# A Strassen-type encoder layer on one core: four turned copies and one row scaling on VectorE, one weight's conversion behind the sums of h, three behind bank copies

## The chip, the core and the metric

One core of a Trainium2 chip runs the whole kernel. It has TensorE (PE in the profile, with PEld for its weight loads), VectorE (DVE), ScalarE (ACT), GpSimd (POOL) and SyncE (SP). Each engine takes its instructions in the order in which they stand and waits for the others by semaphores. The metric is device time in microseconds (us), lower is better.

## The reference, cut to what matters

```python
for l in range(1):                                   # DEPTH 1, x is (1, 512, 2048) float32
    h = rms_norm(x, pre_mix_g)
    z = h @ w_in                                     # q, k, v, u
    m = concatenate([chunked_attention(q, k, v), multiscale_pool(u)]) @ w_o
    x = x + rms_norm(m, post_mix_g)
    h = rms_norm(x, pre_ffn_g)                       # <- the change is here
    up = causal_dwconv(h @ w_up, conv_w, conv_b)     # <- and here; w_up is 2048 x 11264
    y = (gelu(up[..., :5632]) * up[..., 5632:]) @ w_down
    x = x + rms_norm(y, post_ffn_g)
```

All arithmetic is float32.

## The kernel before, in words

**Float32 by two parts.** A float32 operand is split into a rounded part `hi` and the rest `lo`. `split` does it with two instructions: ScalarE copies the source into `hi` (L140, or L143 with a scale), VectorE subtracts `hi` from the source (L141). So each block that is to be multiplied costs one ScalarE and one VectorE instruction on a 128x1024 tile. `split.last` and `split.rest` are those two instructions, and `tc.issue_after(x)` makes what follows stand behind `x` in the order of its engine.

**Seven products.** The large multiplications take seven block products in the place of eight (the Strassen-Winograd form). For `h @ w_up` the 512 tokens make two halves and the 2048 rows of `w_up` make two halves. The columns are taken in groups numbered k = 0 to 42, and each (k, i) with i in 1 to 7 is one product. Products 5, 3 and 6 need sums of the quarters of h; they are made once, in `h_sums` (L1387 to 1407), and serve all k. They need sums of w_up's blocks too: these are made by adding transfers that POOL issues (L1113), the next one for a block as soon as the last sum in it has been split. `Factors` (L1065 to 1159) lists the products in order, loads the blocks and splits them some products ahead (`factors.ahead`). `mm2` (L167 to 183; L170 with `hi`, L176 with `lo`) multiplies: eight matmuls of 512 columns, [hi|lo] of h against the weight's `hi`, and eight of 256 columns, `hi` of h against the weight's `lo`. For products 6, 7 and 4 the narrow ones come first.

**Banks.** Products 1, 6, 7 and 4 of one k add up in one PSUM bank `qa`. After 1, 6 and 7 the bank is copied out (`keep`; `m<-qa` L1438 after product 6, L1444 after product 7), and the next of them may only then go on in it. For k below 4, 5 and 3 go to banks `qg` and `qe`. All eight banks are in use, so a new bank waits until its last reader is done.

**The order around the change.** TensorE's order is written out by hand. The other engines' order comes from a scheduler, which follows the program's order, priorities and `issue_after`. After the attention output is added to x, the rows of x are normalised: `hn[2]` and `hn[3]` are the scaled rows of tokens 256 to 511 (`x` times `rn`). `turn_back` turns them with TensorE: 128x128 transposes into a bank `xt`, and two copies per pair of blocks, with a gain per partition, into `a` tiles (`wholes`), from which `split` makes the factor `gT`. While that goes on, TensorE takes products (0,1), (1,1), (0,2), (2,1), (1,2), (3,1), (2,2), two pairs' transposes, (3,2), and then four pairs' transposes. Then comes one ordinary product `up` (four weights `w_0` to `w_3`, L162 to 165), with the last two pairs' transposes after its first quarter, and then (0,5), (1,5), (0,3), (0,6), (1,3), (0,7), (2,5), (0,4), (1,6), (2,3), (1,7), (3,3), (1,4), (2,6) and on.

During `up`, VectorE and ScalarE make the sums. In `h_sums` the quarters are `a11`, `a21`, `a12`, `a22`, each in two pieces i = 0, 1. `keep(n, i, at, v)` splits a sum into `h<n><i>`, stored in the slot `at` of a pool. Slots are re-used: h3's first piece goes to slot 3, which is where `a22` was; its second piece to slot 2, where `a21` was. In the same place the quarter `a21` is split into `gT0` and `gT1` once more, after its sum was taken. `factors.make_early(0, 6)` splits the weight of product (0, 6) there.

Of the kernel before, what the change touches and what calls it, by code (L numbers as in the profile page):

```python
# [11 lines left out]
AF = mybir.ActivationFunctionType  # L12
# [27 lines left out]
V_PREFFN = V_PREMIX + KD  # L40
# [5 lines left out]
def f32(ap):  # L46
    return ap.bitcast(F32)
# [34 lines left out]
def encoder_layer(ctx: ExitStack, tc: tile.TileContext, x, xT, vecs, rel, post_mix, post_ffn,  # L82
# [7 lines left out]
    nc = tc.nc  # L90
# [15 lines left out]
    def bank(name):  # L106
        return psum.tile([P, 512], F32, tag="ps", name=name)
# [27 lines left out]
    def col(v, i):  # L135
        return vec[:, v + i:v + i + 1]

    def split(hi, lo, src, scale=None):
        if scale is None:
            rounded = nc.scalar.activation(hi, src, AF.Copy)  # L140
            rest = nc.vector.tensor_sub(lo, src, f32(hi))  # L141
        else:
            rounded = nc.scalar.activation(hi, src, AF.Copy, scale=scale)  # L143
            rest = nc.vector.scalar_tensor_tensor(lo, src, scale, f32(hi), op0=ALU.mult, op1=ALU.subtract)
        split.last, split.rest = rounded.ins, rest.ins
        return rounded.ins
# [200 lines left out]
    T = S // 2  # L347
# [12 lines left out]
    for kb in range(KD):  # L360
        i, o = divmod(kb, 8)
# [259 lines left out]
    with tc.tile_pool(name="p1", bufs=2, reuse_waits="tile") as p1:  # L621
# [22 lines left out]
        def project(name, between=None):  # L644
            ps = bank(name)
            for i in range(2):
                if i and between:
                    between()
                w = weights.get(f"{name}_{i}")
                for j in range(8):  # L650
                    kb = 8 * i + j
                    mm3(ps, part(w, j), g_both(hT, kb), kb == 0, kb == KD - 1)
            return ps
# [145 lines left out]
        def mid(h):  # L799
            def step():  # L800
                values(h)
                if h == 2:
                    scores(3)
                elif h + 2 < HEADS:
                    ready_head(h + 2)
                if h == 3:
                    v_load(1)
                more_sums(2 if h in (3, 4) else 1)
            return step

        for j in range(8):
            ps = project(f"u{j}", mid(2 if j == 0 else j + 1) if j not in (1, 7) else None)
# [85 lines left out]
    def h8(n, name, dt=F32):  # L898

        return sums_pool.tile([P, 2048], dt, tag=f"h{n}", name=name)  # L900

    if True:
# [7 lines left out]
        rn = small[:, 32:36]  # L910
# [64 lines left out]
        xn = {}  # L975
# [25 lines left out]
        hn, wholes = {}, {}  # L1001

        def quarter(k, t, i):

            return tuple(hT[2 * k + i][:, :, at, :] for at in AT[t])

        def turn_back(t0, pair, ps):

            for k in range(2):
                kb = 2 * pair + k  # L1010
                for t in range(2):
                    nc.tensor.matmul(ps[:, k * T + t * P:k * T + (t + 1) * P], hn[t0 + t][:, kb * P:(kb + 1) * P],
                                     ident, start=not k and not t, stop=True, is_transpose=True,
                                     skip_group_check=True)
            v = wholes[pair // 4, t0 // 2]
            for k in range(2):
                kb = 2 * pair + k
                nc.scalar.activation(v[:, kb % 8, :], ps[:, k * T:(k + 1) * T], AF.Copy, scale=col(V_PREFFN, kb))
            if pair % 2:
                i = pair // 2 % 2  # L1020
                split(*quarter(pair // 4, t0 // 2, i), v[:, 4 * i:4 * i + 4, :])
# [15 lines left out]
        for t in range(2):  # L1037
            hn[t] = h8(t, f"hn{t}")
            for l in range(2):
                cs = slice(l * D // 2, (l + 1) * D // 2)  # L1040
# [121 lines left out]
        factors = Factors()  # L1162
# [9 lines left out]
            hn[t] = acc8(f"hn{t}", "A")  # L1172
        for l in range(2):
            cs = slice(l * D // 2, (l + 1) * D // 2)
            nc.scalar.activation(hn[2][:, cs], xn[2][:, cs], AF.Copy, scale=rn[:, 2:3])
            nc.vector.tensor_scalar_mul(hn[3][:, cs], xn[3][:, cs], rn[:, 3:4])
        for k in range(2):
            wholes[k, 1] = whole_tile(h8(2 + k, f"a2{k + 1}"))

# [139 lines left out]
    if True:  # L1319
# [9 lines left out]
        def holder(name):  # L1329

            if name not in held:
                v = acc8(name, {"zc": "A", "m8": "A", "x01": "B", "x23": "B"}[name])
                held[name] = parts_of(v, *((512, 512, 1024) if name == "m8" else (1024, 1024)))
            return held[name]
# [37 lines left out]
        T = S // 2  # L1372
# [8 lines left out]
        def raw_x(name):  # L1381
            n = raw_x.n = raw_x.n + 1
            return holder(("x01", "x23")[n // 2 % 2])[n % 2]
# [3 lines left out]
        def h_sums():  # L1387
            def keep(n, i, at, v):
                hs.setdefault(n, {})[i] = h8(at, f"h{n}{i}", F32R).rearrange("p (a b c) -> p a b c", a=4, b=2)
                split(*(hs[n][i][:, :, p, :] for p in range(2)), v)  # L1390

            halves = [[wholes[k, t][:, 4 * i:4 * i + 4, :] for k in range(2) for t in range(2)] for i in range(2)]
            for i, (a11, a21, a12, a22) in enumerate(halves):
                nc.vector.tensor_sub(a22, a22, a21)
                keep(5, i, (1, 0)[i], a22)
                nc.vector.tensor_sub(a21, a11, a21)
                nc.vector.scalar_tensor_tensor(a22, a22, -1.0, a11, op0=ALU.mult, op1=ALU.subtract)
                keep(6, i, (4, 5)[i], a22)
            factors.make_early(1, 5)
            for i, (a11, a21, a12, a22) in enumerate(halves):  # L1400
                nc.vector.scalar_tensor_tensor(a12, a22, -1.0, a12, op0=ALU.mult, op1=ALU.subtract)
            for i in range(2):
                split(*quarter(0, 1, i), halves[i][1])
            for i in range(2):
                keep(3, i, (3, 2)[i], halves[i][2])
                if not i:
                    factors.make_early(0, 6)

        banks, gates = {}, {}

# [5 lines left out]
        def wide(v):  # L1416
            return v.rearrange("p a b c -> p (a b c)")

        def keep(k, i):

            if i == 1:
                banks[k, "d"] = bank(f"qd_{k}")
                keep.copied = nc.scalar.activation(banks[k, "d"], banks[k, "a"], AF.Copy).ins
            elif i == 2:
                v, d = first_parts[:, k % 4, :], banks.pop((k, "d"))
                zs[k, "1"] = v
                nc.scalar.activation(v, d[:, :T], AF.Copy)
                nc.vector.tensor_add(v, d[:, T:], v)
            elif i in (5, 3) and k < 4:
                return  # L1430
            elif i == 5:
                zs[k, "5"] = raw_x("zb")[:, :S] if k == end else holder("m8")[1]
                nc.scalar.activation(zs[k, "5"], banks[k, "g"], AF.Copy)  # L1433
            elif i == 6:
                m = raw_x("zm") if k == end else holder("m8")[2]
                zs[k, "m"] = m.rearrange("p (a b c) -> p a b c", a=2, b=2)
                v = wide(zs[k, "m"][:, :1])
                keep.copied = nc.scalar.activation(v, banks[k, "a"], AF.Copy).ins  # L1438
                nc.vector.tensor_add(v, banks[k, "g"] if k < 4 else banks.pop((k, "g")), v)
                if k < 4:  # L1440
                    nc.vector.tensor_add(v, banks.pop((k, "e")), v)
            elif i == 7:
                v = wide(zs[k, "m"][:, 1:])
                keep.copied = nc.scalar.activation(v, banks[k, "a"], AF.Copy).ins  # L1444
                nc.vector.tensor_add(v, banks.pop((k, "g")) if k < 4 else zs.pop((k, "5")), v)
            elif i == 4:
                keep_all(k)
# [82 lines left out]
        for k, i in factors.order[8 + 4 * PLAIN:]:  # L1530
            seven(k, i)
            keep(k, i)
            if (k, i) == (0, 6):
                factors.behind[0, 4], factors.ahead = keep.copied, factors.AHEAD
                with tc.issue_after(keep.copied):
                    gates[0] = gate(0, first_z)
            if (k, i) in ((2, 7), (5, 1)):
                u, z = zs.pop("late")
                with tc.issue_after(keep.copied):
                    gates[u] = gate(u, z)  # L1540
            if (k, i) == (end, 6):
                summed.close()
                pr = ctx.enter_context(tc.tile_pool(name="pr", bufs=2, side="right", reuse_waits="tile"))
            if (k, i) == (end, 6):
                next_first()
            elif (k, i) == (end - 1, 4):
                next_first()
# [5 lines left out]
    with tc.tile_pool(name="p4", bufs=2, reuse_waits="tile") as p4:  # L1553
# [180 lines left out]
        for n in ("11", "12", "21", "22"):  # L1734
            for t in range(2):
# [3 lines left out]
                if n in not_stored:  # L1739
                    v = at[:, l * C + S:(l + 1) * C]  # L1740
# [60 lines left out]
```

## Time and profile before

| what | value |
|---|---|
| runs | 1855.86, 1857.83 and 8078.94 us; median 1857.83 |
| the profiled execution | 1855.29 us, span 1853.5 us from first to last instruction |
| TensorE | 1838.7 us busy, 99% |
| VectorE, ScalarE, GpSimd | 1463.5, 1127.6, 310.1 us busy |
| mean granted TensorE clock | 0.998 |

The 8078.94 us run is set apart here; the other two and the profiled execution lie within 2.6 us. A row of the timeline is: start, duration, engine, line, operation, tile written <- tiles read, shape, how many merged, and in brackets the idle time before and what ended it. A row of waits is: total us, how often, the longest. A row of stretches is: from, to, length, then busy us of PE, PEld, DVE, ACT, POOL (with counts), the granted clock, the DMA share and GB/s.

### The profile page before, as it was taken

The page shows a single profiled execution, that of the slowest core. Times are in us where ns is not written, and L with a number is a line of the kernel's source. Part 1 is how long each engine was busy: PE and PEld are TensorE (multiplying, and loading weights), DVE is VectorE, ACT ScalarE, POOL GpSimd, SP SyncE. Part 2 cuts the span into 40 slices and gives each one's busy share as a digit, 9 for nine tenths or more (in the row PEclk, how much of TensorE's full clock was granted, in tenths as well). Part 3 has the DMA queues.
Part 4 walks back from the last instruction along what each step waited for, and adds up shares of the span by engine and source line. Part 5 has one row for each costly group of instructions (what it writes and reads, how often), then busy time and mean ns, then how long its engine had stood idle before and what let it go on. Part 6 is the DMA issues. An engine that isn't in the chain of part 4 may idle for free.

```text
span 1853.5 us, 25319 instructions
## 1 busy us (share of the span) xinstructions
PE 1838.7 (99%) x9530; PEld 1579.2 (85%) x9530; DVE 1463.5 (79%) x1698; ACT 1127.6 (61%) x1490; POOL 310.1 (17%) x411
## 2 busy tenths in 40 slices
PE   9999999999999999999999999999999999999998
PEld 7888888888888888888888888888888888888886
DVE  6988778878678787777777777777777899899875
ACT  7655555456587676666666666666665655555553
POOL 3411000100001212212122122221221001111101
PEclk9999999999999999999999999999999999999999
DMA  8599978999979989988888889899888977787785
GB/s 316 172 319 302 319 227 235 276 260 302 349 272 287 228 209 210 198 203 202 205 200 204 206 199 198 202 210 205 197 178 299 360 220 167 193 216 174 176 242 144
DMA packets 139467, 430.21 MB, mean 232 GB/s; under 512 B 12048, under 2 KB 15504, under 8 KB 133648
## 3 DMA queue, kind: packets, MB, share of 16 engines
q0 software_dynamic: 56016, 177.75, 47.9%
q1 hardware_dynamic: 83328, 250.84, 38.4%
q8 instruction: 75, 1.23, 0.3%
q14 instruction: 48, 0.39, 0.1%
HBM read 374.54 MB, written 104.33 MB: 258 GB/s over the span
## 4 chain that ended last, share of the span: by engine, by line
PE 92%; DMA 3%; issue 2%; DVE 1%; ACT 1%; POOL 0%; SPq 0%; DVEq 0%; POOLq 0%; ACTq 0%
PE qa L170 19%; PE qa L176 10%; PE qg L170 9%; PE qg L176 5%; PE qd L170 4%; PE pa L165 4%; PE pa L164 4%; PE pa L162 4%; PE qd L176 2%; PE m L164 2%; PE m L165 2%; PE m L162 2%; PE pg L165 2%; PE pg L164 2%; PE pg L162 2%
## 5 line engine op out<-in xcount | busy, mean ns | idle before, releaser
L170 PE MATMUL qa<-gT,wfh 128*128 128x512 f32 x1200 | 300.4, 392 | 0.0
L141 DVE TENSOR_TENSOR wfl<-x,wfh 128x1024 fp32r<-128x1024 f32 x165 | 202.1, 1225 | 95.0 <-ACT wfh L140 78.0
L170 PEld LDWEIGHTS qa<-gT,wfh 128*128 128x128 f32 x1200 | 215.9, 189 | 38.7
L140 ACT ACTIVATE wfh<-x 128x1024 fp32r<-128x1024 f32 x165 | 174.3, 1056 | 82.5 <-PE qg L170 48.2
L1113 POOL DMA_DIRECT2D x<-in_w_up x125 | 107.2, 860 | 479.1 <-DVE wfl L141 465.6
L176 PE MATMUL qa<-gT,wfl 128*128 128x256 f32 x1200 | 167.8, 283 | 0.8 <-ACT m L1438 0.8
L170 PE MATMUL qg<-h,wfh 128*128 128x512 f32 x656 | 162.2, 389 | 0.2 <-ACT m L1433 0.2
L176 PEld LDWEIGHTS qa<-gT,wfl 128*128 128x128 f32 x1200 | 157.8, 191 | 5.2 <-ACT m L1438 1.0
L141 DVE TENSOR_TENSOR wfl<-wy,wfh 128x1024 fp32r<-128x1024 f32 x100 | 122.0, 1222 | 33.1 <-ACT wfh L140 30.8
L170 PEld LDWEIGHTS qg<-h,wfh 128*128 128x128 f32 x656 | 122.9, 188 | 26.0 <-ACT m L1433 0.6
L140 ACT ACTIVATE wfh<-wy 128x1024 fp32r<-128x1024 f32 x100 | 105.1, 1053 | 63.6 <-PE qd L170 49.7
L141 DVE TENSOR_TENSOR bl<-b,bh 128x2048 fp32r<-128x2048 f32 x56 | 127.1, 2286 | 18.7 <-ACT bh L140 11.7
L140 ACT ACTIVATE bh<-b 128x2048 fp32r<-128x2048 f32 x56 | 106.1, 1913 | 54.6 <-DVE b L1243 22.2
L162 PE MATMUL pa<-bh,ah 128*128 128x512 f32 x320 | 124.5, 389 | 0.0
L164 PE MATMUL pa<-bl,ah 128*128 128x512 f32 x320 | 124.5, 389 | 0.0
L165 PE MATMUL pa<-bh,al 128*128 128x512 f32 x320 | 124.5, 389 | 0.0
L170 PE MATMUL qd<-gT,wfh 128*128 128x512 f32 x400 | 99.0, 390 | 0.0
L176 PEld LDWEIGHTS qg<-h,wfl 128*128 128x128 f32 x656 | 89.5, 190 | 6.4
L176 PE MATMUL qg<-h,wfl 128*128 128x256 f32 x656 | 91.5, 282 | 0.0
L170 PEld LDWEIGHTS qd<-gT,wfh 128*128 128x128 f32 x400 | 74.7, 188 | 15.3
L170 PE MATMUL qa<-h,wfh 128*128 128x512 f32 x344 | 86.1, 392 | 0.0
L141 DVE TENSOR_TENSOR wfl<-wz,wfh 128x1024 fp32r<-128x1024 f32 x50 | 61.2, 1224 | 30.9 <-PE qa L170 28.2
(574 smaller groups left out, 4280.4 us busy)
## 6 DMA issues: line engine op xcount, KB each, us to landing
x<-in_w_up POOLq DMA_DIRECT2D x125, 512.0 KB, 6.3
b<-in_w_down SPq DMA_DIRECT2D x32, 1024.0 KB, 7.0
wt<-in_w_o POOLq DMA_DIRECT2D x24, 1024.0 KB, 15.3
wz<-in_w_up SPq DMA_DIRECT2D x43, 512.0 KB, 5.7
x<-in_w_up SPq DMA_DIRECT2D x43, 512.0 KB, 5.1
wy<-in_w_up SPq DMA_DIRECT2D x43, 512.0 KB, 4.2
wy<-in_w_up POOLq DMA_DIRECT2D x43, 512.0 KB, 6.6
sum<-part POOLq DMA_DIRECT2D x38, 512.0 KB, 7.3
```

The lines of the kernel that those rows point to most:

```text
L140: rounded = nc.scalar.activation(hi, src, AF.Copy)
L141: rest = nc.vector.tensor_sub(lo, src, f32(hi))
L162: nc.tensor.matmul(ps, l[0], r[0], start=first, stop=False, skip_group_check=onto)
L164: nc.tensor.matmul(low, l[0], r[1], start=False, stop=False, skip_group_check=onto)
L165: nc.tensor.matmul(ps, l[1], r[0], start=False, stop=last, skip_group_check=onto)
L170: nc.tensor.matmul(ps, w[0][:, kb], pairs[kb][0], start=fresh and not kb, stop=last, skip_group_check=not fresh)
L176: nc.tensor.matmul(ps[:, sl], w[1][:, kb], pair[:, sl], start=False, stop=last, skip_group_check=not fresh)
L1113: nc.gpsimd.dma_start(self.raw[k, what], self.block(k, m, kh), accum_op=ALU.add)
```

## The change

Three edits:

1. The rows `hn[2]`, which ScalarE scaled, are scaled by VectorE, as `hn[3]` already was. And of the copies out of the turned banks, the second of each pair 0 to 3 goes to VectorE (four copies of 128x256).
2. In `h_sums`, h3's first piece is split ahead of the second splits of `a21`. These are put behind it by `issue_after`, h3's second piece stands behind them, and the weight of (0, 6) behind that.
3. The weight of product 4 is split behind the bank copy of product 6 for k = 0, 1 and 2, which was so for k = 0 alone. Weights are taken three products ahead until k = 2, and four from there on (before: four from k = 0).

```diff
@@ turn_back
-                nc.scalar.activation(v[:, kb % 8, :], ps[:, k * T:(k + 1) * T], AF.Copy, scale=col(V_PREFFN, kb))
+                source = ps[:, k * T:(k + 1) * T]
+                if t0 and pair < 4 and k:
+                    nc.vector.tensor_scalar_mul(v[:, kb % 8, :], source, col(V_PREFFN, kb))
+                else:
+                    nc.scalar.activation(v[:, kb % 8, :], source, AF.Copy, scale=col(V_PREFFN, kb))
@@ rows of hn
-            nc.scalar.activation(hn[2][:, cs], xn[2][:, cs], AF.Copy, scale=rn[:, 2:3])
-            nc.vector.tensor_scalar_mul(hn[3][:, cs], xn[3][:, cs], rn[:, 3:4])
+            for t in range(2, 4):
+                nc.vector.tensor_scalar_mul(hn[t][:, cs], xn[t][:, cs], rn[:, t:t + 1])
@@ h_sums
+            keep(3, 0, 3, halves[0][2])
             for i in range(2):
-                split(*quarter(0, 1, i), halves[i][1])
-            for i in range(2):
-                keep(3, i, (3, 2)[i], halves[i][2])
-                if not i:
-                    factors.make_early(0, 6)
+                with tc.issue_after(split.last), tc.issue_after(split.rest):
+                    split(*quarter(0, 1, i), halves[i][1])
+            keep(3, 1, 2, halves[1][2])
+            with tc.issue_after(split.last), tc.issue_after(split.rest):
+                factors.make_early(0, 6)
@@ the loop over the products
             keep(k, i)
+            if i == 6 and k < 3:
+                factors.behind[k, 4], factors.ahead = keep.copied, factors.AHEAD - (k < 2)
             if (k, i) == (0, 6):
-                factors.behind[0, 4], factors.ahead = keep.copied, factors.AHEAD
```

TensorE's, POOL's and SyncE's instructions stand in the same order before and after. ScalarE's and VectorE's move at three places, which are shown as built. Names such as `h30` are h3's first piece, `h31` its second, `wfh` and `wfl` a weight's `hi` and `lo`, `zc` and `m8` tiles for finished columns.

First, VectorE while the rows are turned (`first_parts` frees a bank that a product 2 used; `xt2`, `xt3` are the third and fourth turned pairs):

```order
 L141 TENSOR_TENSOR gT0_4822<-a21_5256,gT0_4822 128x4x256
 L141 TENSOR_TENSOR w00_1l_5503<-w00_1r_5217,w00_1h_5502 128x1024
-L1428 TENSOR_TENSOR first_parts_5274<-qd_3_5409,first_parts_5274 128x256
+L1433 TENSOR_TENSOR first_parts_5274<-qd_3_5409,first_parts_5274 128x256
+L1020 TENSOR_SCALAR a21_5256<-xt2_5463,vec_69 128x256
+L1020 TENSOR_SCALAR a21_5256<-xt3_5470,vec_69 128x256
 L141 TENSOR_TENSOR gT1_4823<-a21_5256,gT1_4823 128x4x256
 L141 TENSOR_TENSOR w00_2l_5550<-w00_2r_5294,w00_2h_5549 128x1024
```

The copies of xt2 and xt3 are new on VectorE. The sixth pair's transposes waited for a ScalarE copy before, and wait for VectorE now (`first_parts<-qd_3` above).

Second, VectorE at the end of the sums, before and then after, with the semaphores that each row waits for:

```order
L1401 SCALAR_TENSOR_TENSOR a12_5003<-a22_5257,a12_5003 128x1024
L141 TENSOR_TENSOR h61_5607<-a22_5257,h61_5607 128x4x256 [waits Activation_49]
L1401 SCALAR_TENSOR_TENSOR a12_5003<-a22_5257,a12_5003 128x1024
L141 TENSOR_TENSOR gT0_4822<-a21_5256,gT0_4822 128x4x256
L141 TENSOR_TENSOR gT1_4823<-a21_5256,gT1_4823 128x4x256
L141 TENSOR_TENSOR h30_5621<-a12_5003,h30_5621 128x4x256 [waits Activation_49]
L141 TENSOR_TENSOR wfl_5625<-wx_5150,wfh_5624 128x1024 [waits DMASW0_49,PE_49]
L141 TENSOR_TENSOR h31_5629<-a12_5003,h31_5629 128x4x256 [waits Activation_49]
```

```order
L1405 SCALAR_TENSOR_TENSOR a12_5003<-a22_5257,a12_5003 128x1024
L1405 SCALAR_TENSOR_TENSOR a12_5003<-a22_5257,a12_5003 128x1024 [waits DVE_49]
L141 TENSOR_TENSOR h61_5607<-a22_5257,h61_5607 128x4x256 [waits Activation_49]
L141 TENSOR_TENSOR h30_5617<-a12_5003,h30_5617 128x4x256 [waits Activation_49]
L141 TENSOR_TENSOR gT0_4822<-a21_5256,gT0_4822 128x4x256 [waits Activation_49]
L141 TENSOR_TENSOR gT1_4823<-a21_5256,gT1_4823 128x4x256 [waits Activation_49]
L141 TENSOR_TENSOR h31_5624<-a12_5003,h31_5624 128x4x256 [waits Activation_49]
L141 TENSOR_TENSOR wfl_5628<-wx_5150,wfh_5627 128x1024 [waits DMASW0_49,PE_49,Activation_49]
```

The two splits of gT moved from ahead of h30 to between h30 and h31, and the weight `wfl` of (0, 6) from ahead of h31 to behind it. ScalarE's `hi` parts follow: before, it made the two of gT long ahead, and `wfh` of (0, 6) stood between the two copies `zc<-up`, ahead of h30; now the row is `zc`, `zc`, h30, gT0, gT1, h31, `wfh` of (0, 6).

Third, ScalarE around the bank copy of product (1, 6), `m8<-qa_1`, before and after (`wfh_5892` and `wfh_5911` are the weight of (1, 4)):

```order
L1454 ACTIVATE zc_5686<-qa_0_5275 128x256 [waits PE_49]
L140 ACTIVATE wfh_5892<-x01_5497 128x1024 [waits DMASW0_49,DVE_49,PE_49]
L1323 ACTIVATE m8_5772<-zc_5686,vec_69 128x512 [waits DVE_49]
L1438 ACTIVATE m8_5772<-qa_1_5300 128x512 [waits PE_49]
L140 ACTIVATE wfh_5917<-x01_5497 128x1024 [waits DMASW7_49,PE_49,Activation_49]
```

```order
L1459 ACTIVATE zc_5686<-qa_0_5275 128x256 [waits PE_49]
L1327 ACTIVATE m8_5772<-zc_5686,vec_69 128x512 [waits DVE_49]
L1443 ACTIVATE m8_5772<-qa_1_5300 128x512 [waits PE_49]
L140 ACTIVATE wfh_5911<-x01_5497 128x1024 [waits DMASW0_49]
L1457 ACTIVATE zc_5686<-first_parts_5274 128x256 [waits DVE_49,Activation_49]
```

The weight of (1, 4), which waits for a transfer (`DMASW0`), moved from ahead of the bank copy to behind it.

## The prediction

> **What bounds the kernel now.** The page's first part says who is busy, and a split of the span into stretches says where TensorE is not.
>
> ```profile
> PE 1838.7 (99%) x9530; PEld 1579.2 (85%) x9530; DVE 1463.5 (79%) x1698; ACT 1127.6 (61%) x1490; POOL 310.1 (17%) x411
> 565.00:650.00 85.00, 82.29 (x439) 70.59 (x438) 67.97 (x75) 58.43 (x80) 18.55 (x21) 0.98 1.01 260
> 650.00:1800.00 1150.00, 1149.83 (x6102) 994.44 (x6101) 913.40 (x900) 713.42 (x868) 207.10 (x238) 1.00 0.86 210
> ```
>
> TensorE bounds it. All three edits act between 565 and 650 us, and nothing that TensorE executes is removed. There it is idle for 85.00 - 82.29 = 2.7 us, against 0.2 us in the 1150 us behind it, and the granted clock is 0.98 there, 1.00 behind it. The waits of TensorE in this stretch name who is late:
>
> ```profile
> PE qe L170 <- DVE h L141: 1.7, 2, 1.0
> PE qa L176 <- ACT m L1438: 0.8, 1, 0.8
> ```
>
> They are h3's two pieces on VectorE and the bank copy of (1, 6) on ScalarE. TensorE's timeline gives what each costs, by starts, since ends overlap:
>
> ```profile
> 573.71 1.47 PE L1012 MATMUL xt<-ident,hn 128*128 128x128 f32 x12
> 575.34 0.66 PE L1012 MATMUL xt<-ident,hn 128*128 128x128 f32 x4 [0.16 <-ACT a L1018]
> 601.64 2.00 PE L170 MATMUL qg<-h,wfh 128*128 128x512 f32 x8
> 603.48 1.11 PE L176 MATMUL qg<-h,wfl 128*128 128x256 f32 x8
> 605.29 1.17 PE L170 MATMUL qe<-h,wfh 128*128 128x512 f32 x4 [0.70 <-DVE h L141]
> 607.47 2.08 PE L170 MATMUL qe<-h,wfh 128*128 128x512 f32 x4 [1.01 <-DVE h L141]
> 609.35 1.79 PE L176 MATMUL qe<-h,wfl 128*128 128x256 f32 x8
> 610.97 1.12 PE L176 MATMUL qa<-h,wfl 128*128 128x256 f32 x8
> 629.51 1.11 PE L176 MATMUL qe<-h,wfl 128*128 128x256 f32 x8
> 631.38 1.22 PE L176 MATMUL qa<-gT,wfl 128*128 128x256 f32 x8 [0.77 <-ACT m L1438]
> 632.44 2.00 PE L170 MATMUL qa<-gT,wfh 128*128 128x512 f32 x8
> ```
>
> Eight wide matmuls take 603.48 - 601.64 = 1.84 us, eight narrow ones 0.95, twelve transposes 1.31. So (0, 3) could start at 604.44 and starts at 605.29 (0.85 lost). Its second four could start 0.92 later, at 606.21, and start at 607.47 (1.26 lost). Then four wide ones take 1.88 and eight narrow ones 1.62 where 0.92 and 0.95 are usual: 1.63 lost to the clock. (1, 7) starts at 631.38 in place of 630.46, and its narrow ones take 1.06: 1.0 lost. At 575 the sixth pair loses 0.32, and `up` behind it about 0.24. Together 5.3 us, or 0.3% of the kernel: the most that this change can give.
>
> **Edit 1: work from ScalarE to VectorE.** ScalarE loses two scalings and four copies; VectorE takes them:
>
> ```profile
> 566.04 2.19 ACT L1175 ACTIVATE hn<-x,small 128x1024 f32<-128x1024 f32 x2 [0.52 <-POOL small L999]
> 570.68 1.57 ACT L1018 ACTIVATE a<-xt,vec 128x256 f32<-128x256 f32 x4
> 566.04 1.42 DVE L1176 TENSOR_SCALAR hn<-x,small 128x1024 f32<-128x1024 f32 x2 [0.81 <-POOL small L999]
> 573.38 1.23 DVE L141 TENSOR_TENSOR gT<-a,gT 128x1024 fp32r<-128x1024 f32 x1 [2.29 <-ACT gT L140]
> 574.52 1.22 DVE L141 TENSOR_TENSOR w_1l<-w_1r,w_1h 128x1024 fp32r<-128x1024 f32 x1
> 575.66 0.42 DVE L1428 TENSOR_TENSOR first_parts<-qd,first_parts 128x256 f32<-128x256 f32 x1
> 579.40 1.23 DVE L141 TENSOR_TENSOR w_2l<-w_2r,w_2h 128x1024 fp32r<-128x1024 f32 x1 [0.81 <-ACT w_2h L140]
> ```
>
> Two more scalings cost VectorE 1.4 us at 567, ahead of the transposes at 570. A copy from a bank to VectorE with a gain is not in this stretch. I take 0.42, from the row of `first_parts` (same shape, also from a bank); the bounds are 0.39 (ScalarE's, 1.57 / 4) and 0.60 (`m<-qa` on ScalarE, twice the width, below). VectorE's idle times of 2.29 and 0.81 hide them, so they cost it nothing.
>
> What gets later is a bank. By the order, the sixth pair waits for VectorE now, behind `w_1l` and `first_parts`. One copy on ScalarE ends at about 571.2, VectorE's two follow by 572.05, and the split of gT0 begins some 0.2 us sooner than before. So `first_parts` comes at 575.48 and ends at 575.90. The sixth pair starts there in place of 575.34, four transposes take 0.44, and `up` starts at 576.4. Before, the steps from 575.34 and 0.24 put it at 576.07. **Cost: 0.33 us later.** With the two copies at 0.60 each it would be 0.7, at 0.39 0.3; at best, with the banks free in time, the 0.56 lost here would go. ScalarE is ready for `w_2h` no sooner, since the same late pair's copies stand ahead of it. So I let VectorE's row from 579.40 on start where it did.
>
> **Edit 2: h3 ahead of the second splits.** From 579.40 VectorE hardly stops:
>
> ```profile
> 599.97 1.22 DVE L1401 SCALAR_TENSOR_TENSOR a<-a,a 128x1024 f32<-128x1024 f32 x1
> 601.11 2.35 DVE L141 TENSOR_TENSOR gT<-a,gT 128x1024 fp32r<-128x1024 f32 x2
> 603.92 1.23 DVE L141 TENSOR_TENSOR h<-a,h 128x1024 fp32r<-128x1024 f32 x1 [0.46 <-ACT h L140]
> 605.06 1.22 DVE L141 TENSOR_TENSOR wfl<-wx,wfh 128x1024 fp32r<-128x1024 f32 x1
> 606.20 1.22 DVE L141 TENSOR_TENSOR h<-a,h 128x1024 fp32r<-128x1024 f32 x1
> 601.39 1.06 ACT L140 ACTIVATE wfh<-wx 128x1024 fp32r<-128x1024 f32 x1 [2.40 <-DMA wx<-in_w_up]
> 602.83 2.00 ACT L140 ACTIVATE h<-a 128x1024 fp32r<-128x1024 f32 x2
> ```
>
> Before: ScalarE sat 2.40 us behind the transfer of (0, 6)'s weight, so h30's `hi` came at 602.83, and VectorE used the time for the two splits of gT. After: up to the end of h61, VectorE does the same nineteen instructions as before up to 601.19. But h30 is stored where a22 was, and h61 is the last that reads a22. So ScalarE begins h30's `hi` at 601.2 and VectorE, whose next instruction is h30's `lo`, stands still until 602.3. It ends h30 at 603.5, in time for TensorE. The two splits of gT end at 605.8. h31 is stored where a21 was, which these splits read, so its `hi` starts then, 1.06 more, and its `lo` runs from 606.9 to 608.1. The order took 1.14 (the weight) out of the row and put two waits of about 1.1 us into it, which the splits of gT covered before. TensorE reaches (0, 3) at 604.44 + 0.33 = 604.77, does four matmuls, and waits from 605.69 to 608.15. **Cost: 608.15 in place of 607.47, 0.68 later**; the 0.33 is inside this. Behind VectorE's waiting instruction stand the weights of (0, 6), (1, 3), (0, 7). The first is ready at 609.25, and TensorE needs it at 608.15 + 1.87 = 610.0: no cost.
>
> Then the clock. The second wait for h3 was followed by a half-speed stretch; the one other wait of about this length was not:
>
> ```profile
> 478.97 0.50 PE L164 MATMUL m<-wo_3l,s 128*128 128x512 f32 x1 [0.94 <-DVE wo_3l L141]
> 475.00:483.00 8.00, 7.06 (x32) 5.51 (x31) 5.95 (x6) 7.54 (x10) 0.00 (x0) 1.00 0.82 285
> 604.00:611.00 7.00, 5.29 (x22) 4.21 (x22) 5.69 (x5) 3.89 (x4) 1.72 (x2) 0.76 0.86 177
> ```
>
> Idle 0.94 alone left the clock at 1.00; 0.70 and 1.01 close together took it to 0.76 over 7 us, (1 - 0.76) x 7 = 1.7 us. One wait of 2.4 us holds more idle time than those two, so I let the 1.63 stay. The bounds are 0 and 1.63. [...]
>
> **Edit 3: product 4's weights.**
>
> ```profile
> 607.11 0.86 POOL L1113 DMA_DIRECT2D wx<-in_w_up  x1 [8.17 <-DVE wfl L141]
> DMA to landing us min/median/max: 8.4/11.8/15.1
> 619.53 0.60 ACT L1444 ACTIVATE m<-qa 128x512 f32<-128x512 f32 x1 [0.76 <-PE qa L170]
> 629.09 1.06 ACT L140 ACTIVATE wfh<-x 128x1024 fp32r<-128x1024 f32 x1 [3.48 <-DMA x<-in_w_up]
> 630.05 0.80 ACT L1323 ACTIVATE m<-zc,vec 128x512 f32<-128x512 f32 x1
> 630.76 0.57 ACT L1438 ACTIVATE m<-qa 128x512 f32<-128x512 f32 x1
> 626.90 0.42 DVE L1455 TENSOR_TENSOR zc<-qa,zc 128x256 f32<-128x256 f32 x1
> ```
>
> ScalarE waited 3.48 us for the transfer into (1, 4)'s weight with the bank copy of (1, 6) behind it. Now the copy stands ahead. It still stands behind a chain that begins with (0, 4)'s weight. That weight's adding transfer is issued after (0, 6)'s `lo`, 609.25 in place of 606.28: at 610.1 in place of 607.11. It lands at 618.5 with the 8.4 us that it took (the 15.1 are those of the transfer that ScalarE waited for until 601.39). On ScalarE follow `wfh`, `zc`, `wfh` and the copy of (0, 7), which ends at 621.4; (0, 4) is due at 622.10 + 0.68 = 622.8. Behind it come a table load, the gelu, three weights on both engines and `zc`, which took from 619.53 + 0.60 = 620.13 to 626.90 + 0.42 = 627.32, or 7.2 us, and then the convolution step (0.80) and the copy itself (0.57). So the copy of (1, 6) ends at 621.4 + 8.6 = 630.0; (1, 7) is due at 630.46 + 0.68 = 631.1. **Gain: 1.0 us**, with 1.1 us to spare. POOL and SyncE keep their order, so no queue is passed. Weights taken one product later have 2.8 us each to hide in.
>
> **The sum.** 1855.29 + 0.68 + 0 - 1.0 = 1855.0 us, on the profiled execution (span 1853.5 and 1.8 around it). The two other runs shown lie 0.57 and 2.54 above it, and their median with the third is the higher one; I add 1.0 and say **1856.0**.
>
> **Rivals**, all with the 1.0 added. (a) The sums come in time: ScalarE, 3.6 us freer, lets VectorE's row start 2.4 us sooner. Then 0.85, 1.26, 1.63 and 1.0 go and 0.33 comes: 1851.9. For it: VectorE's idle 2.29 and 0.81. Against: only 0.81 lies at the row's start, and the two new waits. (b) The clock stays full behind one wait, as it did at 479. TensorE is then 1.63 us sooner, the 1.1 us to spare are gone and 0.5 of the wait at 631 is back: 1856.0 - 1.63 + 0.5 = 1854.9. [...] (c) **Slower**: (0, 4)'s weight, issued 3 us later among others, lands after 15.1 us, as the other one into `wx` did. (0, 4) then waits 6.7 - 1.4 = 5.3 us, and the clock halves again: 1863. It decides from 8.4 + 1.4 = 9.8 us to landing. (d) Edit 3 doesn't do what it says: the copy is ahead of the weight, but its convolution step comes late and (1, 7) waits as before: 1857.0.
>
> Chances: forecast 0.5, (a) 0.14, (b) 0.16, (c) 0.08, (d) 0.12. The range 1851.5 to 1860 takes in all but (c). All cases lie within 2% (37 us), which is about what a measurement of this kernel tells from no change: same 0.97, faster 0.01, slower 0.02.
>
> **What would show it.** One wait of `qe` on `h` of about 2.3 us in place of two; the granted clock at about 0.76 behind it; VectorE idle twice for about 1.1 us before `h`; `xt` waiting for VectorE's `first_parts`; no wait of `qa` on L1443. Wrong would be: no wait of `qe` (a), a clock of 1.00 there (b), or `qa` waiting near 622 (c).

## The result and the profile after

| | before, beside it | after |
|---|---|---|
| median | 1858.8 us (14 runs) | 1853.82 us (14 runs, 1851.81 to 1857.21) |
| ratio | | 0.9974, 95% interval 0.9961 to 0.9986 |
| profiled execution | 1855.29 us, span 1853.5 | 1856.03 us, span 1854.2 |

One run of before, of 8078.94 us, is left out of the ratio. The change is worth 4.8 us (2.6 to 7.2), which is within 2%. The two profiled executions alone say the opposite, +0.74 us: that of before is near the low end of its runs, that of after near the high end. So the traces are read here for where the waits are, and the medians for what the change is worth.

First the page of the kernel after, and its stretches:

```profile
PE 1838.0 (99%) x9530; PEld 1578.9 (85%) x9530; DVE 1466.1 (79%) x1704; ACT 1123.7 (61%) x1484; POOL 310.1 (17%) x411
565.00:650.00 85.00, 81.90 (x444) 70.80 (x443) 71.45 (x81) 55.22 (x75) 18.55 (x21) 0.98 1.02 261
650.00:1800.00 1150.00, 1148.26 (x6092) 992.93 (x6091) 912.72 (x899) 712.43 (x866) 207.09 (x238) 1.00 0.85 210
```

In 565 to 650 VectorE is 3.5 us busier (67.97 before), ScalarE 3.2 less (58.43), and TensorE hardly changed (82.29 before). In the 1150 us behind it TensorE is busy 1.6 us less than before (1149.83), most of it by the wait of 1.4 us on L1443 below.

TensorE's waits in the kernel after, and its timeline at the places of the prediction:

```profile
PE qe L170 <- DVE h L141: 2.3, 1, 2.3
PE qa L176 <- ACT m L1443: 1.4, 1, 1.4
PE xt L1012 <- DVE first_parts L1433: 0.8, 1, 0.8
```

```profile
575.85 0.66 PE L1012 MATMUL xt<-ident,hn 128*128 128x128 f32 x4 [0.81 <-DVE first_parts L1433]
604.61 1.09 PE L170 MATMUL qe<-h,wfh 128*128 128x512 f32 x4
608.00 2.07 PE L170 MATMUL qe<-h,wfh 128*128 128x512 f32 x4 [2.29 <-DVE h L141]
609.87 1.66 PE L176 MATMUL qe<-h,wfl 128*128 128x256 f32 x8
611.36 1.11 PE L176 MATMUL qa<-h,wfl 128*128 128x256 f32 x8
629.89 1.12 PE L176 MATMUL qe<-h,wfl 128*128 128x256 f32 x8
630.85 1.12 PE L176 MATMUL qa<-gT,wfl 128*128 128x256 f32 x8
```

One wait for h3 stands where two were, the sixth pair waits for VectorE, and (1, 7) at 630.85 has no wait. The wait of `qa` on L1443 in the list is another, at 679.80, where (4, 7) stands behind a ScalarE that waits 3.38 us for a transfer of finished columns (`gd<-zc`). The second profile of the kernel before, below, has 1.02 us there too, so this wait is not the change's alone.

VectorE and ScalarE of the kernel after show why:

```profile
575.71 0.87 DVE L1020 TENSOR_SCALAR a<-xt,vec 128x256 f32<-128x256 f32 x2
602.10 1.23 DVE L141 TENSOR_TENSOR h<-a,h 128x1024 fp32r<-128x1024 f32 x1 [1.12 <-ACT h L140]
603.24 2.35 DVE L141 TENSOR_TENSOR gT<-a,gT 128x1024 fp32r<-128x1024 f32 x2
606.72 1.23 DVE L141 TENSOR_TENSOR h<-a,h 128x1024 fp32r<-128x1024 f32 x1 [1.12 <-ACT h L140]
607.86 1.22 DVE L141 TENSOR_TENSOR wfl<-wx,wfh 128x1024 fp32r<-128x1024 f32 x1
```

```profile
601.01 1.06 ACT L140 ACTIVATE h<-a 128x1024 fp32r<-128x1024 f32 x1 [1.16 <-DVE h L141]
605.63 1.06 ACT L140 ACTIVATE h<-a 128x1024 fp32r<-128x1024 f32 x1 [1.67 <-DVE gT L141]
617.82 1.06 ACT L140 ACTIVATE wfh<-wx 128x1024 fp32r<-128x1024 f32 x1 [1.47 <-DMA wx<-in_w_up]
628.80 0.57 ACT L1443 ACTIVATE m<-qa 128x512 f32<-128x512 f32 x1
630.03 1.06 ACT L140 ACTIVATE wfh<-x 128x1024 fp32r<-128x1024 f32 x1 [0.65 <-DMA x<-in_w_up]
```

Each piece of h3 is a chain between the two engines with nothing beside it: VectorE frees the slot, ScalarE writes `hi` into it (1.06), VectorE subtracts. VectorE therefore stands still for 1.12 us twice. The copy of (1, 6) ends at 629.37, 1.5 us ahead of its reader, and the weight that held it up before stands behind it.

### The profile page after: what moved, and what is told of

Same layout as the page of the kernel before. It is cut to its first block, busy times and chain, and to the rows that moved or that the text cites. A ratio compares the mean times of both kernels' runs of the same rounds, so it can differ in the third digit from the quotient of the medians.

```text
span 1854.2 us, 25307 instructions
## 1 busy us (share of the span) xinstructions
PE 1838.0 (99%) x9530; PEld 1578.9 (85%) x9530; DVE 1466.1 (79%) x1704; ACT 1123.7 (61%) x1484; POOL 310.1 (17%) x411
## 4 chain that ended last, share of the span: by engine, by line
PE 93%; DVE 2%; DMA 2%; issue 1%; ACT 1%; POOL 0%; SPq 0%; DVEq 0%; POOLq 0%; ACTq 0%
PE qa L170 19%; PE qa L176 10%; PE qg L170 9%; PE qg L176 5%; PE qd L170 5%; PE pa L162 4%; PE pa L164 4%; PE pa L165 4%; PE m L164 3%; PE m L165 3%; PE m L162 3%; PE qd L176 2%; PE pg L162 2%; PE pg L164 2%; PE pg L165 2%; PE v L165 2%
```

## The experiments

The first four kernels below share one chip and its runs of the kernel before. The kernel after once more, the two without sums and the first run with the splits ahead share a second, the other four a third. Ratios are against the runs of before on the same chip; behind each stands its 95% interval.

**The kernel before once more** (no edit).

> The kernel before, unchanged, profiled once more. Transfer theory: its profiled execution was a lucky one; here ScalarE waits longer than 2.4 us and 3.5 us for the transfers into the weights of (0, 6) and (1, 4), and TensorE waits more than 1.7 us for h3 or more than 0.8 us for the bank copy of (1, 6). Rival (fixed gain: the two kernels differ by the same amount in every execution): the waits of TensorE between 565 and 650 us are those of the first profile within 0.3 us.

It took 1859.7 us, where the median of before on this chip was 1856.01 (29 runs, 1853.78 to 1861.8). Its TensorE and its ScalarE at the end of the sums:

```profile
601.37 1.11 PE L176 MATMUL qg<-h,wfl 128*128 128x256 f32 x8
604.68 1.15 PE L170 MATMUL qe<-h,wfh 128*128 128x512 f32 x4 [2.21 <-DVE h L141]
606.86 2.07 PE L170 MATMUL qe<-h,wfh 128*128 128x512 f32 x4 [1.03 <-DVE h L141]
```

```profile
600.79 1.06 ACT L140 ACTIVATE wfh<-wx 128x1024 fp32r<-128x1024 f32 x1 [3.91 <-DMA wx<-in_w_up]
```

The second wait is the same as in the first profile (1.01). The first is 2.21 in place of 0.70, and ScalarE's wait for the transfer of (0, 6)'s weight is 3.91 in place of 2.40: both 1.5 more. The transfer itself was not late: ScalarE has the weight at 600.79 here and at 601.39 in the first profile, and from issue to landing the transfer took 15.8 and 15.1 us. It is TensorE that came sooner. It is ready for (0, 3) at 601.37 + 0.95 = 602.32 here and at 604.44 in the first profile, and the 2.1 us are there at the sixth pair already (573.24 and 575.34). In both profiles (0, 3) starts 3.9 us after ScalarE got the weight. So what the kernel before loses at h3 depends on how far TensorE is ahead of that transfer, and the prediction was made against an execution in which TensorE came late. The other half of the expectation failed: ScalarE's wait for the weight of (1, 4) is 2.52 us, less than 3.48, and (1, 7) does not wait.

**Each edit alone.** Edit 1 (its added lines; the scaled rows stand in a loop over t):

```diff
+                if t0 and pair < 4 and k:
+                    nc.vector.tensor_scalar_mul(v[:, kb % 8, :], source, col(V_PREFFN, kb))
+                    nc.vector.tensor_scalar_mul(hn[t][:, cs], xn[t][:, cs], rn[:, t:t + 1])
```

> Edit 1 alone (rows of hn and four copies on VectorE). Transfer theory: no gain, -0.5 to +0.5 us; the sixth pair waits about 0.9 us for VectorE in place of 0.56, and the waits for h3 and for the bank copy stay. Rival (ScalarE's relief is the gain): 3 to 5 us faster than before.

1856.72 us, ratio 0.9998 (0.9990 to 1.0007): nothing. The later sixth pair is there (`xt` waits 0.8 us for `first_parts`), and the order at h3 is still that of before:

```profile
604.42 1.15 PE L170 MATMUL qe<-h,wfh 128*128 128x512 f32 x4 [1.42 <-DVE h L141]
```

Edit 2:

```diff
+            keep(3, 0, 3, halves[0][2])
             for i in range(2):
-                split(*quarter(0, 1, i), halves[i][1])
-            for i in range(2):
-                keep(3, i, (3, 2)[i], halves[i][2])
-                if not i:
-                    factors.make_early(0, 6)
+                with tc.issue_after(split.last), tc.issue_after(split.rest):
+                    split(*quarter(0, 1, i), halves[i][1])
+            keep(3, 1, 2, halves[1][2])
+            with tc.issue_after(split.last), tc.issue_after(split.rest):
+                factors.make_early(0, 6)
```

> Edit 2 alone (h3 ahead of the second splits, the weight of (0, 6) behind). Transfer theory: slower by 1 to 4 us, since one wait of 2.3 to 3 us for h3 stays, everything behind it is later, and the wait of (1, 7) behind (1, 4)'s transfer grows from 0.8 to over 2 us. Rival (edit 2 is the gain, as the first transfer no longer holds up h3): 3 to 5 us faster.

1857.21 us, ratio 1.0007 (0.9997 to 1.0017): nothing, or a little slower. Its waits:

```profile
PE qe L170 <- DVE h L141: 2.8, 1, 2.8
PE qa L176 <- ACT m L1439: 2.7, 1, 2.7
```

The single wait is 2.8, not 2.3, and the wait of (1, 7) is still there, and longer than the 0.8 of before. This profile is of the slowest of its 12 runs (1864.32).

Edit 3:

```diff
+            if i == 6 and k < 3:
+                factors.behind[k, 4], factors.ahead = keep.copied, factors.AHEAD - (k < 2)
             if (k, i) == (0, 6):
-                factors.behind[0, 4], factors.ahead = keep.copied, factors.AHEAD
```

> Edit 3 alone (product 4's weights behind the bank copies). Transfer theory: 1 to 4 us faster, since the wait of (1, 7) is gone however late the transfer is; the two waits for h3 and the half clock stay. Rival (edit 2 or 1 is the gain): within 1 us of before.

1854.06 us, ratio 0.9987 (0.9979 to 0.9996), or 2.4 us less (0.7 to 3.9). (1, 7) has no wait, and the two waits for h3 remain:

```profile
605.05 1.17 PE L170 MATMUL qe<-h,wfh 128*128 128x512 f32 x4 [1.74 <-DVE h L141]
607.23 2.08 PE L170 MATMUL qe<-h,wfh 128*128 128x512 f32 x4 [1.01 <-DVE h L141]
```

Of the three, edit 3 alone is a gain by itself. Edit 1 alone and edit 2 alone are not.

**The kernel after once more** (no edit).

> The changed kernel, unchanged, against before on one chip. Transfer theory: 1.5 to 4 us faster than before by the medians; in its profile the wait for h3 is again one of 2.2 to 2.6 us (VectorE's order sets it, no transfer), and (1, 7) waits under 0.3 us. Rival (fixed gain, or none): within 1 us of before, or the wait for h3 moves by over 0.5 us between the two profiles of this kernel.

1854.09 us (12 runs, 1852.58 to 1855.08) beside 1858.11 (31 runs, 1853.31 to 1864.13): ratio 0.9979 (0.9970 to 0.9988), or 3.9 us less. The gain repeats on a second chip. The times lie closer together too: 2.5 us from lowest to highest here, though over fewer runs, and 10.8 before; on the first chip 5.4 and 15.7. The wait at h3 is what it was:

```profile
606.41 2.07 PE L170 MATMUL qe<-h,wfh 128*128 128x512 f32 x4 [2.30 <-DVE h L141]
```

**Without the sums in w_up's blocks.** The six adding transfers of k = 0 to 2 are left out, in the kernel before and in the kernel after, so that no split waits for one of them. The weights of products 6 and 4 of these k are then not the sums:

```diff
-                elif i == 5:
+                elif i == 5 and k >= 3:
                     self.add(k, "x", 1, 1)
-                elif i == 6:
+                elif i == 6 and k >= 3:
                     self.add(k, "x", 0, 1)
```

> Before, with the adding transfers behind products 5 and 6 of k = 0, 1 and 2 left out (six transfers of 512 KB; the weights of products 6 and 4 of these k are then not the sums), so that ScalarE never waits for them. Transfer theory: ScalarE's waits of 2.4 and 3.5 us are gone, (1, 7) waits under 0.3 us, the first wait for h3 shrinks to under 0.9 us, and the kernel is 2 to 4 us faster than before. Rival (order of the engines, not transfers): within 1 us of before.

> After, with the same six transfers left out (the same weights are then not the sums). Transfer theory: the wait for h3 stays at 2.2 to 2.6 us, and the kernel is within 1.5 us of after: the change has taken these transfers off the path. Rival (transfers cost both kernels the same): as much faster than after as the kernel before gets by the same cut.

Before without them: 1852.79 us, ratio 0.9978 (0.9968 to 0.9987). After without them: 1853.22 us, ratio 0.9977 (0.9967 to 0.9988), against 0.9979 for the kernel after as it is, on the same chip. So the six transfers cost the kernel before 4.1 us (2.4 to 5.9), and the kernel after nothing that can be measured. That the kernel after gains nothing speaks against a mere relief of the other transfers as the cause. In the kernel before without them, the first wait for h3 is down to 0.31 by starts (the trace names none), and the second remains:

```profile
PE qe L170 <- DVE h L141: 1.0, 1, 1.0
```

(1, 7) has no wait and the clock stays at 1.00 there, so TensorE loses 3.1 and 4.8 us less between 565 and 660 than in the two profiles of the kernel before. The 4.1 us of the times lie between the two.

In the kernel after without them, the one wait stays at 2.31:

```profile
603.82 1.09 PE L170 MATMUL qe<-h,wfh 128*128 128x512 f32 x4
607.22 1.20 PE L170 MATMUL qe<-h,wfh 128*128 128x512 f32 x4 [2.31 <-DVE h L141]
608.26 1.10 PE L176 MATMUL qe<-h,wfl 128*128 128x256 f32 x8
```

This wait is the chain between VectorE and ScalarE, whatever the transfers do.

**Edits in pairs.** Edits 1 and 3 (the diffs of the first and the third kernel above together), then 2 and 3:

> After without edit 2 (h_sums as before). If edit 2 pays by taking the transfer of (0, 6)'s weight out of h3's way: slower than after, 0.9985 to 1.000 of before, with two waits for h3 whose first differs from 0.85 us by how late that transfer is. Rival (edit 2 swaps one wait for another of equal size): as fast as after, 0.997 to 0.9985 of before.

> After without edit 1. If edit 1 only moves the sixth pair's wait: 0.997 to 0.9985 of before, as after; a wait of 0.3 us at the sixth pair, one of 2.8 to 3.0 us for h3, none over 0.3 us at (1, 7). Rival (edit 2 needs ScalarE's relief): 0.9985 or above.

Edits 1 and 3: 1853.97 us, ratio 0.9985 (0.9977 to 0.9994), the sum of the two alone (0.9998 and 0.9987). It lies on the border of the two expectations and does not decide between them. Edits 2 and 3: 1855.34 us, ratio 0.9995 (0.9986 to 1.0004), also the sum of the two alone (1.0007 and 0.9987). This is on the side of the rival, that edit 2 needs ScalarE's relief. With all three it is 0.9974 and 0.9979. By these medians edit 2 costs a little without edit 1 and gains a little with it. Part of that is in the trace of edits 2 and 3:

```profile
PE qe L170 <- DVE h L141: 2.7, 1, 2.7
```

Without edit 1 the wait for h3 is 2.9 us by starts (edit 2 alone, edits 2 and 3), with it 2.5 (three profiles). That is 0.4 us; the ratios differ by 3 to 4 us, with intervals that touch or overlap. The rest isn't found in single profiles.

**The splits of gT ahead of h3.** If the wait is the bare chain, other work of VectorE beside ScalarE's `hi` must hide it. From the kernel after:

```diff
-            keep(3, 0, 3, halves[0][2])
             for i in range(2):
-                with tc.issue_after(split.last), tc.issue_after(split.rest):
-                    split(*quarter(0, 1, i), halves[i][1])
-            keep(3, 1, 2, halves[1][2])
+                split(*quarter(0, 1, i), halves[i][1])
+            for i in range(2):
+                keep(3, i, (3, 2)[i], halves[i][2])
             with tc.issue_after(split.last), tc.issue_after(split.rest):
                 factors.make_early(0, 6)
```

> After, with the second splits of a21 put back ahead of h3's first piece (the weight of (0, 6) stays behind h3). Theory of the two uncovered waits of VectorE: h30's lo ends at about 604.4 and h31's at 605.6, TensorE waits under 0.4 us for h3, the clock stays at 1.00 there, and the kernel is 2.5 to 4 us faster than after. Rival (the sums are bound by VectorE's work, not by its order): the wait stays above 1.5 us and the time within 1 us of after. Second rival (time won here is waited for again at the transfer into (0, 4)'s weight): h3 is in time and the kernel less than 1.5 us faster than after.

> The kernel with the second splits of a21 ahead of h3 and all three edits, again, beside the other three on one chip: 0.995 to 0.998 of before, 2 to 4 us faster than the kernel with edits 1 and 3 and than the kernel with edits 2 and 3; no wait for h3, clock at 1.00 between 565 and 650 us. Rival (its first measurement was chance): within 1 us of those two.

1851.76 us, ratio 0.9966 (0.9953 to 0.9979), and on another chip 1851.78 us, ratio 0.9973 (0.9963 to 0.9984). Beside the kernel after on the first of these chips it is 2.3 us less, a little short of the 2.5 to 4 expected, and the intervals overlap. Beside edits 2 and 3 on the second it is 3.6 us less, and beside edits 1 and 3 it is 2.2 less. From edits 1 and 3 it differs in one thing alone: the weight of (0, 6), with its wait for the transfer, stands behind h3. So taking that weight out of h3's way pays by these medians (the intervals overlap here too), and putting the splits of gT between the pieces of h3, the other part of edit 2, gives about as much back. VectorE, TensorE and the stretch in the second run:

```profile
597.82 1.21 DVE L141 TENSOR_TENSOR h<-a,h 128x1024 fp32r<-128x1024 f32 x1
598.95 2.35 DVE L141 TENSOR_TENSOR gT<-a,gT 128x1024 fp32r<-128x1024 f32 x2
601.23 2.43 DVE L141 TENSOR_TENSOR h<-a,h 128x1024 fp32r<-128x1024 f32 x2
603.58 1.22 DVE L141 TENSOR_TENSOR wfl<-wx,wfh 128x1024 fp32r<-128x1024 f32 x1
```

```profile
602.66 2.25 PE L170 MATMUL qe<-h,wfh 128*128 128x512 f32 x8
604.75 1.10 PE L176 MATMUL qe<-h,wfl 128*128 128x256 f32 x8
625.60 1.22 PE L176 MATMUL qa<-gT,wfl 128*128 128x256 f32 x8 [0.16 <-ACT m L1442]
```

```profile
565.00:650.00 85.00, 84.04 (x464) 72.65 (x464) 74.52 (x84) 57.50 (x76) 17.89 (x20) 1.00 1.02 262
```

VectorE runs h61, gT0, gT1, h30, h31 and the weight without a stop, TensorE does the eight matmuls of (0, 3) in one piece, and the clock stays at 1.00. From 600 to 614, TensorE loses 0.31 us against its usual steps, where the kernel after lost 4.00. Not all of the 3.7 us come out in the time: TensorE is sooner at the next products, and from 614 to 660 it loses 1.02 where the kernel after lost 0.14, among it the 0.16 above. At (4, 7), near 675, it loses another 0.8, where the two profiles of the kernel after lose 1.7 and nothing.

The same order without edit 1 (the lines of the copies; the scaled rows are as before too):

```diff
-                source = ps[:, k * T:(k + 1) * T]
-                if t0 and pair < 4 and k:
-                    nc.vector.tensor_scalar_mul(v[:, kb % 8, :], source, col(V_PREFFN, kb))
-                else:
-                    nc.scalar.activation(v[:, kb % 8, :], source, AF.Copy, scale=col(V_PREFFN, kb))
+                nc.scalar.activation(v[:, kb % 8, :], ps[:, k * T:(k + 1) * T], AF.Copy, scale=col(V_PREFFN, kb))
```

> The kernel with the second splits of a21 ahead of h3, without edit 1. If edit 1 pays nothing: as the same kernel with edit 1, 0.995 to 0.998 of before; waits at the sixth pair of 0.3 us and for h3 under 0.8 us in all, clock at 1.00. Rival (edit 1 frees ScalarE for the sums): waits for h3 over 1 us and at least 1 us slower than with edit 1.

1852.89 us, ratio 0.9982 (0.9972 to 0.9992). It is 1.1 us above the kernel with edit 1, within the intervals, and just outside the 0.995 to 0.998 expected. The wait for h3 is 0.15 us, so in this profile the sums do not need edit 1. TensorE waits 1.33 us for a bank copy at 654.93 in this profile, and 0.12 there with edit 1; whether edit 1 does that, and what it is worth here, is not settled.

## Why the prediction was right, and which term was mis-sized

The time, 1853.82, lies 2.2 us below the forecast of 1856.0, and inside its range. The waits stand where it put them. By its own steps, in the profile of the kernel after:

- **Edit 1.** The sixth pair was to start at 575.90 and starts at 575.85. Two copies from a bank on VectorE take 0.87 to 0.92, where 0.84 was put in.
- **Edit 2.** h30's `lo` was to begin at 602.3 and begins at 602.10. The splits of gT were to end at 605.8; they end at 605.6. h31 begins at 606.72 in place of 606.9, and TensorE goes on at 608.00 in place of 608.15. The weight of (0, 6) is ready at 609.08, ahead of its reader at 609.87, so it costs nothing, as said.
- **The clock.** The half clock came again behind the one wait (0.50 from 607.68 to 611.09): matmuls from 608.00 to 611.36 take 3.36 us where 1.87 is usual, a loss of 1.49; 1.63 was put in. Rival (b), by which it would go, did not occur here or in the second profile of after. It did in the kernel after without the six transfers and with edit 2 alone, as the last section shows.
- **Edit 3.** (0, 4)'s weight was to land at 618.5; ScalarE took it at 617.82. The copy of (1, 6) ends at 629.37 (forecast 630.0), and (1, 7) starts without a wait at 630.85 (forecast 631.1). Rivals (c) and (d) did not occur. Nor did (a): the sums were not in time. Its 3.6 us of relief for ScalarE are 3.76 by its rows (2.19 and 1.57), and ScalarE is 3.2 us less busy in the stretch.

Together TensorE's loss from 565 to 660 went from 5.7 to 5.2 us, 0.5 less where 0.3 was forecast. As a description of these two executions, the sum holds. As a price of the change it does not.

**The term that was mis-sized** is the gain, and with it the start of the sum. The sum starts at 1855.29 + 1.0 = 1856.3 us, and the kernel before measures 1858.8, or 2.5 more. Its gain is 0.3 us, and 4.8 were measured, or 4.5 more. The two misses point opposite ways; that the time came within 2.2 us of the forecast is in part luck. Both were taken from one profiled execution, with ScalarE's waits of 2.40 and 3.48 us for transfers taken as fixed. They are not fixed.

In five profiles with the order of before at h3 (before, its second profile, edit 1 alone, edit 3 alone, edits 1 and 3) the first wait for h3 is 0.86, 2.36, 1.58, 1.90 and 1.16 us by starts, 1.57 on average; without the transfers it is 0.31. The second is 1.26 in each. In all five TensorE starts (0, 3) 3.9 us after ScalarE got the weight of (0, 6), and this transfer took 15.1 to 15.8 us from issue to landing, while the time at which TensorE was ready varies by 2.1 us. So much of the time that TensorE wins ahead of h3 is lost again at h3. With the order of after and edit 1 it is one wait of 2.46 to 2.48, with transfers or without. So edits 1 and 2 together take h3 from a mean of 2.83 to 2.47, 0.4 less, where the one profile of before shows 0.35 more (2.11 to 2.46). With the half clock behind these waits counted in, it is again 0.4, by the two profiles of after.

The wait of (1, 7) too is a spread: 0.8, none, 1.0 and 2.7 us in the four profiles without edit 3 that have the transfers. In each of the four, (1, 7) starts 2.3 us after ScalarE got the weight of (1, 4).

That the gain has to do with the transfers is shown by leaving them out: the kernel before gains 4.1 us by it, as much as by the change, and the kernel after gains nothing more. Which of the six transfers counts for how much was not tried.

**What stays open** is where all of it lies. By the profiles of this stretch the change is worth 0.4 us at h3, 1.1 on average at (1, 7), less 0.3 at the sixth pair: 1.2 us, against a measured 3.9 and 4.8 (intervals 2.2 to 5.6 and 2.6 to 7.2). Edit 3 alone measures 2.4, twice its mean wait, though 1.1 lies inside its interval. Elsewhere single profiles differ by more than that: between 1340 and 1400 us TensorE loses 0.64 in the profile of before and 3.89 in its second. The kernel after without the six transfers has that loss too (2.80 us of idle time at 1370.36), so the change does not do away with it. Whether it makes it rarer was not tried.

## What to carry to other kernels

Before a wait for a transfer is put into a sum, see it in more than one execution: here it grew as TensorE came sooner, and was 0.86 us in one profile and 2.36 in another. The mean of several is a better price than the value of one, though here even the means leave most of the gain open. Where a piece of work passes from one engine to another and back, keep independent work of the first engine beside it; here two splits that were ready hid ScalarE's part, 1.06 us for each piece, when they stood ahead of h3, and the clock stayed at 1.00; when they stood between its pieces, they left a wait of 2.3 us, and the clock went to 0.50 for 3.41 us in both profiles of the kernel after. A gain in one stretch is to be followed to the next one, since TensorE sooner is also sooner at the next late transfer: here its loss from 600 to 614 went from 4.00 to 0.31 us, and that from 614 to 660 from 0.14 to 1.02.

## What the runs showed of the clock

At h3 the granted clock is 0.50 for 3.41 us in the profile of the kernel before and in that of the kernel after. Each of these stretches, with the 3.41 us ahead of it (TensorE's busy time is the number behind the comma, the granted clock the third from the end):

```profile
604.03:607.44 3.41, 1.73 (x9) 1.03 (x7) 3.41 (x4) 2.80 (x3) 0.33 (x1) 1.00 1.02 202
607.44:610.85 3.41, 3.38 (x12) 3.00 (x13) 2.25 (x2) 1.06 (x1) 1.40 (x2) 0.50 0.69 145
```

```profile
604.27:607.68 3.41, 1.44 (x9) 0.91 (x7) 2.29 (x3) 2.05 (x3) 0.00 (x0) 1.00 0.91 181
607.68:611.09 3.41, 3.09 (x10) 2.71 (x11) 3.41 (x4) 2.83 (x3) 1.45 (x2) 0.50 0.63 196
```

And the kernel after without the six transfers, whose wait is as long, in two stretches of the same length:

```profile
602.61:606.02 3.41, 2.30 (x14) 1.71 (x12) 2.29 (x3) 1.74 (x3) 0.00 (x0) 1.00 0.00 0
606.02:609.43 3.41, 2.21 (x14) 2.02 (x15) 3.41 (x4) 3.41 (x4) 0.00 (x0) 1.00 0.26 83
```

In the kernel before, 1.68 us of idle time in the stretch ahead, in the two waits for h3, are followed by 3.41 us at 0.50, which cost 1.63 us by starts. In the kernel after it is 1.97 us, of the one wait of 2.29, and the half clock behind it costs 1.49. The second profile of the kernel after, with a wait of 2.30, shows the same: 1.97 us of idle time from 602.67 to 606.08, and a clock of 0.50 from 606.08 to 609.49. In the kernel after without the transfers, 1.11 and 1.20 us of idle time lie in the two stretches, and the clock is 1.00 in both and in the 3.42 us behind them. So waits of 2.29, 2.30 and 2.31 us were followed by half clock twice and once not: the length of the wait alone doesn't decide whether it costs some 1.5 us more.

The other profiles do not settle it. With edit 2 alone, the clock is 1.00 over 565 to 650, though TensorE waits 2.75 us for h3 and 2.7 us at (1, 7) there. In the second profile of before, with waits of 2.21 and 1.03 us for h3, it is 0.64 over 604 to 611, where the first profile has 0.76. What decides it was not shown.

Rival (b) was thus not a matter of whether there were one or two waits: behind one, the clock went to 0.50 in both profiles of the kernel after, and stayed at 1.00 in the kernel after without the transfers and with edit 2 alone.
